# Up products of three feed-forwards by seven instead of eight block products, with the hidden values kept in DRAM until a separate down product

## Chip, cores and metric

The kernel runs on one core of a Trainium2 chip: TensorE (PE in the profile; PEld is its weight load) multiplies, VectorE (DVE), ScalarE (ACT) and GpSimd (POOL) do the elementwise work, SyncE (SP) issues most DMAs. Each engine takes its instructions in an order fixed when the program is built. The metric is the time of one execution on the device in microseconds (us), as the median of several runs.

## What is computed

Two transformer blocks in float32 on 1024 tokens of width 1024. Three feed-forwards of hidden width 2816 (22 tiles of 128) stand in it; the change touches these alone:

```
# block 1
h = rms_norm(x, g_pre_ffn[l]) * (1.0 + sc_f) + sh_f
up = dwconv3(h @ w_up[l], conv_w[l], conv_b[l])     # width 3 over the tokens
gate, val = jnp.split(up, 2, axis=-1)
y = (jax.nn.gelu(gate) * val) @ w_down[l]
x = x + gt_f * rms_norm(y, g_post_ffn[l])
# block 2, with ffn1 before its attention and ffn2 after it
def swiglu(x, w_gu, w_down):
    g, u = jnp.split(x @ w_gu, 2, axis=-1)
    return (jax.nn.silu(g) * u) @ w_down
h = h + 0.5 * rms_norm_2(f, ffn1_post_g[i])
```

Around them stand block 1's mixers (state space, Fourier, window attention), block 2's attention and its last gate (`ple`).

## The kernel before

Every float32 product is made of split pairs: a value is hi (rounded to the matmul's float32 format, `split`, by ACT) plus lo (the rest, by DVE), and `mm3` (L82) adds hi·hi, hi·lo and lo·hi in PSUM, so a product of 128x128 by 128x512 is three matmuls.

The activation h lies with its channels on the partitions, by token half: `hT` is two pairs of tiles [128, 8 k-tiles, 512 tokens]. `ffn` (L170) goes over the hidden width in groups of two tiles. A tile needs a gate and a value column block of 128 (`load_up`, one load of 512 KB, split on ACT and DVE), each for two token halves: four products of 8 k-tiles, 96 matmuls (`up`, `piece`). ACT applies silu (L241) or, in block 1, three taps and gelu (L184 to L205), DVE multiplies by the value and the result is split into `hidh`, `hidl` (L244, L206). The down product of the group before is put between the up products: `down` (L259) makes, for each of eight token tiles and two column halves, six matmuls in one PSUM bank, and DVE adds the bank to `yacc` in SBUF (L270). So hidden values never leave the core.

At its start the first two tiles' products are made by quarters of 256 tokens (`quarters`, L95), since h arrives token tile by token tile from the phase before, by transposes (L166) and splits (`hl<-tp` in the rows). At its end the down product of the last group completes the token tiles one by one; in between stand a few late up pieces. Each token tile then goes through `finish`: mean square on ACT (L126), multiplication by a row of gains on POOL (L132), a Newton iteration for the reciprocal root on DVE in 128x1 operations (L110 to L117), the residual (L1677), the next norm (L139) and its transposes.

The order in which the engines take the instructions is set by the program's scheduler from data dependences and from the rings of buffers: `wh`, `wl` a ring of four pairs for weights, `raw` a ring of three for loads, `mm` six PSUM banks.

## Time and profile before

| | |
|---|---|
| runs shown, us | 3457.92, 3458.81, 3458.82; median 3458.81 |
| span of the profiled execution, us | 3453.3; the runs' times hold some 5.5 us around it |
| PE busy | 3285.5 us, 95% of the span |
| DVE, ACT, POOL busy | 1849.3, 1060.3, 385.0 us |
| first feed-forward (block 1), about | 546 to 1255 us |
| second, third | 1309 to 2020, 2595 to 3300 us |

A row of the timeline gives the start of an instruction in us from the span's start, its length, engine, line, operation and tiles. A row of the windows gives for each engine the busy time and the number of instructions in a stretch, then the clock granted to TensorE as a share of full speed. A row of the groups gives the count, the busy time and the mean length of one in ns, then the engine's idle time before them and what ended it.

### The profile page before, as it was taken

Reading aid. Unit: us, or ns where it says so; the run is one execution under the profiler, and the core shown is the slowest. Engines: PE = TensorE matmul, PEld = TensorE weight load, DVE = VectorE, ACT = ScalarE, POOL = GpSimd, SP = SyncE. Lnnn points to the kernel's source line nnn. Section 1 sums busy time; section 2 is a strip of 40 time slices with the busy share of each in tenths; the row PEclk is TensorE's granted clock in tenths of the full one; section 3 lists DMA queues with packets and bytes.
Section 4 is the critical chain, followed back from the end, with each engine's and each line's share of the span. In section 5 each row is a group of like instructions: output and inputs, shape, how many; then the busy total and the mean of one; then the engine's idle time right before and its main releaser. Section 6 shows DMA issues by size and latency. Waiting matters only on the chain. (4 is left out here: it accounts for less than half of the span.)

```text
span 3453.3 us, 40957 instructions
## 1 busy us (share of the span) xinstructions
PE 3285.5 (95%) x16082; PEld 2648.9 (77%) x16082; DVE 1849.3 (54%) x3594; ACT 1060.3 (31%) x1717; POOL 385.0 (11%) x639
## 2 busy tenths in 40 slices
PE   5989888999999989999999989999999999999988
PEld 2766668888888878888888878777779888888866
DVE  7667497455554575233433387667673333333386
ACT  4335534322222223211111135446623111111142
POOL 3478331000000010000000020000020000000022
PEclk8999999999999999999999999999999999999999
DMA  7663543111111123111111132111632111111134
GB/s 204 178 216 116 171 162 119 43 49 49 48 38 55 49 92 98 46 47 49 43 49 49 49 116 85 43 47 66 227 110 74 49 49 49 49 46 47 43 134 146
DMA packets 263092, 293.67 MB, mean 85 GB/s; under 512 B 33448, under 2 KB 206760, under 8 KB 262899
## 3 DMA queue, kind: packets, MB, share of 16 engines
q1 hardware_dynamic: 254434, 276.52, 25.3%
q10 hardware_dynamic: 6576, 9.00, 0.8%
q0 software_dynamic: 1888, 5.53, 0.7%
q8 instruction: 127, 2.08, 0.3%
q14 instruction: 67, 0.54, 0.1%
HBM read 240.24 MB, written 57.06 MB: 86 GB/s over the span
## 5 line engine op out<-in xcount | busy, mean ns | idle before, releaser
L85 PE MATMUL mm<-hh,wh 128*128 128x512 f32 (+1 forms) x2800 | 1057.9, 378 | 15.7 <-ACT hh L47 15.7
L86 PE MATMUL mm<-hl,wh 128*128 128x512 f32 (+1 forms) x2800 | 1056.5, 377 | 3.5 <-DVE hl L48 3.5
L87 PE MATMUL mm<-hh,wl 128*128 128x512 f32 (+1 forms) x2800 | 1055.8, 377 | 0.8 <-DVE wl L48 0.8
L85 PEld LDWEIGHTS mm<-hh,wh 128*128 128x128 f32 x2800 | 529.6, 189 | 118.6 <-ACT hh L47 15.9
L86 PEld LDWEIGHTS mm<-hl,wh 128*128 128x128 f32 x2800 | 529.8, 189 | 105.5 <-DVE hl L48 3.9
L87 PEld LDWEIGHTS mm<-hh,wl 128*128 128x128 f32 x2800 | 529.7, 189 | 104.9 <-DVE wl L48 1.0
L270 DVE TENSOR_TENSOR y<-y,mm 128x512 f32<-128x512 f32 x480 | 324.0, 685 | 215.9 <-PE mm L87 215.5
L48 DVE TENSOR_TENSOR wl<-raw,wh 128x1024 fp32r<-128x1024 f32 x176 | 216.4, 1229 | 395.6 <-ACT wh L47 395.0
L85 PE MATMUL mm<-wdh,hidh 128*128 128x512 f32 x1056 | 414.6, 393 | 7.7 <-DVE tmp L190 5.8
L86 PE MATMUL mm<-wdl,hidh 128*128 128x512 f32 x1056 | 413.9, 392 | 0.0
L87 PE MATMUL mm<-wdh,hidl 128*128 128x512 f32 x1056 | 413.0, 392 | 0.0
L47 ACT ACTIVATE wh<-raw 128x1024 fp32r<-128x1024 f32 x178 | 188.1, 1058 | 604.8 <-PE mm L86 380.8
L243 DVE TENSOR_TENSOR tmp<-tmp,mm 128x512 f32<-128x512 f32 x88 | 60.4, 688 | 478.5 <-PE mm L87 477.4
L132 POOL TENSOR_TENSOR y<-y,row 128x1024 f32<-128x1024 f32 x24 | 59.3, 2475 | 2240.0 <-ACT junk L126 1516.8
L85 PEld LDWEIGHTS mm<-wdh,hidh 128*128 128x128 f32 x1056 | 199.0, 189 | 53.2 <-issue 6.6
L86 PEld LDWEIGHTS mm<-wdl,hidh 128*128 128x128 f32 x1056 | 199.3, 189 | 43.1 <-DVE wdl L48 0.2
L87 PEld LDWEIGHTS mm<-wdh,hidl 128*128 128x128 f32 x1056 | 198.7, 188 | 43.3
L47 ACT ACTIVATE wdh<-raw 128x1024 fp32r<-128x1024 f32 x66 | 66.8, 1054 | 419.8 <-issue 303.4
L47 ACT ACTIVATE hidh<-tmp 128x512 fp32r<-128x512 f32 (+2 forms) x111 | 78.8, 711 | 376.7 <-DVE tmp L243 230.0
L431 ACT ACTIVATE S<-S,m 128x257 f32<-128x257 f32 (+10 forms) x176 | 108.8, 620 | 93.6 <-DVE m L426 86.3
L132 POOL TENSOR_TENSOR tmp<-tmp,row 128x1024 f32<-128x1024 f32 x23 | 59.7, 2601 | 624.4 <-ACT junk L126 557.3
L116 DVE SCALAR_TENSOR_TENSOR rs_t<-rs_i,rs_a 128x1 f32<-128x1 f32 x288 | 124.7, 446 | 3.6
(332 smaller groups left out, 3915.6 us busy)
## 6 DMA issues: line engine op xcount, KB each, us to landing
raw<-in_ffn_w_gu SPq DMA_DIRECT2D x88, 512.0 KB, 3.9
raw<-in_w_ada SPq DMA_DIRECT2D x48, 512.0 KB, 3.8
raw<-in_w_up SPq DMA_DIRECT2D x44, 512.0 KB, 3.9
raw<-in_ffn_w_down SPq DMA_DIRECT2D x44, 512.0 KB, 3.8
x<-tmp SPq DMA_DIRECT2D x40, 512.0 KB, 2.6
tmp<-x SPq DMA_DIRECT2D x40, 512.0 KB, 5.1
raw<-in_w_in SPq DMA_DIRECT2D x28, 512.0 KB, 3.9
mix<-mix SPq DMA_DIRECT2D x44, 256.0 KB, 2.3
```

The source lines that it names most:

```text
L47: self.nc.scalar.activation(hi, src, AF.Copy)
L48: (eng or self.nc.vector).tensor_tensor(lo, src, f(hi), op=OP.subtract)
L85: mm(out, a[0], b[0], start=start, stop=False)
L86: mm(out, a[0], b[1], start=False, stop=False)
L87: mm(out, a[1], b[0], start=False, stop=stop)
L116: v.scalar_tensor_tensor(t, y, s, y, op0=OP.mult, op1=OP.mult)
L132: self.nc.gpsimd.tensor_tensor(y, y, row, op=OP.mult)
L243: v.tensor_tensor(s[:, c], s[:, c], p, op=OP.mult)
L270: v.tensor_tensor(yacc[i][:, c], yacc[i][:, c], po, op=OP.add)
L431: nc.scalar.activation(S[s][:, :ne], S[s][:, :ne], AF.Exp, scale=-1.0, bias=m[:, s:s + 1], accum_out=sm[:, s:s + 1])
```

## The change

`ffn` treats the first two hidden tiles as before, by quarters, but stores their hidden values in DRAM. Then it forms, once per call, sums of quarters of h. With the eight k-tiles in an upper and a lower half (A11, A12 for the first token half, A21, A22 for the second) these are S1 = A21 + A22, S2 = S1 - A11, S3 = A11 - A21 and S4 = A12 - S2, each split into hi and lo; POOL restores the quarters by adding hi and lo (L254), DVE makes the sums (L255 to L258), and S4 takes the place of A21. S1 to S3 lie in new tiles (`S`).

For each of the other 20 tiles the gate and the value block are loaded, POOL forms T1 to T4 from them (L268 to L277), and B11, B21, T1, T2, B22, T3 and T4 are split. Seven products of 4 k-tiles x 3 matmuls (`prod`, L287) go into three PSUM banks, A, B and C; bank A is copied out (ACT L319, L332) or read (DVE L338) between the products that it accumulates. T4's product of a tile is placed after B11's product of the next (`finish_tile`). The activation and the product of gate and value follow, and the hidden tile is stored in DRAM (L311).

When all are done, the down product runs as a phase of its own: pairs of hidden tiles and their weight rows are loaded and split (`load`), 96 matmuls per pair and a DVE add per bank (L368); the first pair is copied by ACT (L366). The last down takes four tiles at once, 24 matmuls per bank, and completes the token tiles one by one. Scratch tiles come from one ring of twelve (`b4`), rows and the sums `yacc` from the ring `S`; `ple` gets its weights' places from both.

```diff
-        return pool.tile([P, D], F32, name="tmp", tag="tmp", bufs=self.tmps)
+        return pool.tile([P, D], F32, name="tmp", tag=self.tmptag, bufs=self.tmps)
+    def places(self, pool, tag, n):
+        self.tmptag, self.tmps = tag, n
+    def count(self):
+        self.counted += 1
+        return self.counted
...
-def ffn(k, hT, w_gu, w_down, nff, prep, finish, G=2, taps=None, then=None):
...
+def ffn(k, hT, w_gu, w_down, nff, prep, finish, taps=None, then=None):
+    nc, v, pool = k.nc, k.nc.vector, k.nc.gpsimd
     with k.tc.tile_pool(name="ffn", bufs=1) as fp:
-        prep(fp)
-        yacc = [fp.tile([P, D], F32, name=f"y{i}") for i in range(NT)]
-        groups = [list(range(a, min(a + G, nff))) for a in range(0, nff, G)]
+        k.places(fp, "b4", 12)
+        hidden = k.dr.tile([nff, P, D], F32, name=f"hidden{k.count()}")
+        def b4(dt=F32):
+            return fp.tile([P, D], dt, name="b4", tag="b4", bufs=12)
+        def big(shape, dt):
+            return fp.tile([P] + shape, dt, name="S", tag="S", bufs=3)
+        state = {}
         def conv_half(U, p, m, h, edge):
...
+        def piece(j, part, h, p):
+            st = state.setdefault(j, {"left": 4})
...
+            c = slice(h * 512, h * 512 + 512)
...
+                if part not in st:
+                    st[part] = b4()
...
+                conv_half(st[part], p, j + part * nff, h, st[part, "e"])
+                if not st["left"]:
+                    s = st[0]
+                    nc.scalar.activation(s, s, AF.Gelu_apprx_tanh)
+                    v.tensor_tensor(s, s, st[1], op=OP.mult)
...
+                if "s" not in st:
+                    st["s"] = b4()
+                s = st["s"]
+                if part == 0:
+                    nc.scalar.activation(s[:, c], p, AF.Silu)
+                else:
+                    v.tensor_tensor(s[:, c], s[:, c], p, op=OP.mult)
+            if not st["left"]:
+                nc.sync.dma_start(hidden[j], s)
+        jobs = ((0, 0), (0, 1), (1, 0), (1, 1))
+        ws = [k.load_up(w_gu, (j + part * nff) * P) for j, part in jobs]
+        for h in range(2):
+            for x, ps in zip(jobs, k.quarters(ws, hT, h)):
+                piece(*x, h, ps)
+        (h0, l0), (h1, l1) = hT
+        sums = [big([2, 4, 512], F32R) for _ in range(3)]
+        up, dn = slice(0, 4), slice(4, 8)
+        A11, A12, A22, S4 = (h0[:, up], l0[:, up]), (h0[:, dn], l0[:, dn]), (h1[:, dn], l1[:, dn]), (h1[:, up], l1[:, up])
+        S1, S2, S3 = [(t[:, 0], t[:, 1]) for t in sums]
+        for a in range(0, 4, 2):
+            c = slice(a, a + 2)
+            x21, x22, x11, x12 = xs = [b4().rearrange("p (a b) -> p a b", a=2) for _ in range(4)]
+            for x, (hi, lo) in zip(xs, (S4, A22, A11, A12)):
+                pool.tensor_tensor(x, f(hi[:, c]), f(lo[:, c]), op=OP.add)
+            v.tensor_tensor(x22, x21, x22, op=OP.add)
+            v.tensor_tensor(x21, x11, x21, op=OP.subtract)
+            v.tensor_tensor(x11, x22, x11, op=OP.subtract)
+            v.tensor_tensor(x12, x12, x11, op=OP.subtract)
+            for x, (hi, lo) in ((x22, S1), (x11, S2), (x21, S3), (x12, S4)):
+                k.split(hi[:, c], lo[:, c], x)
+        def weights(j):
+            rg, rv = k.raw([P, 8, P]), k.raw([P, 8, P])
+            nc.sync.dma_start(rg, w_gu[:, j * P:j * P + P].rearrange("(k p) n -> p k n", p=P))
+            nc.sync.dma_start(rv, w_gu[:, (j + nff) * P:(j + nff) * P + P].rearrange("(k p) n -> p k n", p=P))
+            T = b4().rearrange("p (k n) -> p k n", k=8)
+            pool.tensor_tensor(T[:, up], rv[:, up], rg[:, up], op=OP.subtract)
+            W1 = [w.rearrange("p (k n) -> p k n", k=8) for w in k.wide()]
+            k.split(*W1, rg)
+            pool.tensor_tensor(T[:, dn], rv[:, dn], T[:, up], op=OP.subtract)
+            pool.tensor_tensor(rv[:, up], rv[:, dn], rv[:, up], op=OP.subtract)
+            W2 = [w.rearrange("p (k n) -> p k n", k=8) for w in k.wide()]
+            k.split(*W2, T)
+            W3 = [w.rearrange("p (k n) -> p k n", k=8) for w in k.wide()]
+            k.split(*W3, rv)
+            pool.tensor_tensor(T[:, up], rg[:, dn], T[:, dn], op=OP.subtract)
+            t4 = b4(F32R).rearrange("p (a k n) -> p a k n", a=2, k=4)
+            k.split(t4[:, 0], t4[:, 1], T[:, up])
+            both = lambda W, c: (W[0][:, c], W[1][:, c])
+            return dict(B11=both(W1, up), B21=both(W1, dn), T1=both(W2, up), T2=both(W2, dn), T3=both(W3, up),
+                        B22=both(W3, dn), T4=(t4[:, 0], t4[:, 1]))
+        def prod(ps, w, x, start):
+            for a in range(4):
+                for n, (y, z) in enumerate(((0, 0), (0, 1), (1, 0))):
+                    nc.tensor.matmul(ps, w[y][:, a], x[z][:, a], start=start and a == 0 and n == 0, stop=a == 3 and n == 2,
+                                     skip_group_check=True)
+        lo, hi = slice(0, 512), slice(512, 1024)
+        def finish_tile(j, A, w, s, V):
+            prod(A, w["T4"], A22, False)
+            if taps is None:
+                nc.scalar.activation(s[:, hi], A, AF.Silu)
+                v.tensor_tensor(s[:, hi], s[:, hi], V[:, hi], op=OP.mult)
+            else:
+                nc.scalar.activation(s[:, hi], A, AF.Copy)
+                us = []
+                for m, z in ((j, s), (j + nff, V)):
+                    u = b4()
+                    t = [taps[:, a, m:m + 1] for a in range(4)]
+                    nc.scalar.activation(u, z, AF.Identity, bias=t[3], scale=t[1])
+                    v.scalar_tensor_tensor(u[:, 1:], z[:, :D - 1], t[0], u[:, 1:], op0=OP.mult, op1=OP.add)
+                    v.scalar_tensor_tensor(u[:, :D - 1], z[:, 1:], t[2], u[:, :D - 1], op0=OP.mult, op1=OP.add)
+                    us.append(u)
+                s = us[0]
+                nc.scalar.activation(s, s, AF.Gelu_apprx_tanh)
+                v.tensor_tensor(s, s, us[1], op=OP.mult)
+            nc.sync.dma_start(hidden[j], s)
+        prev = None
+        for j in range(2, nff):
+            w = weights(j)
+            A, B, C = k.mm(), None, None
+            X = b4()
+            prod(A, w["B11"], A11, True)
+            nc.scalar.activation(X[:, lo], A, AF.Copy)
+            if prev is not None:
+                finish_tile(*prev)
+            s, V = b4(), b4()
+            B = k.mm()
+            prod(B, w["B21"], A12, True)
+            v.tensor_tensor(s[:, lo], B, X[:, lo], op=OP.add)
+            if taps is None:
+                nc.scalar.activation(s[:, lo], s[:, lo], AF.Silu)
+            C = k.mm()
+            prod(C, w["T1"], S1, True)
+            nc.scalar.activation(X[:, hi], C, AF.Copy)
+            prod(A, w["T2"], S2, False)
+            nc.scalar.activation(X[:, lo], A, AF.Copy)
+            prod(C, w["B22"], S4, False)
+            v.tensor_tensor(V[:, lo], C, X[:, lo], op=OP.add)
+            if taps is None:
+                v.tensor_tensor(s[:, lo], s[:, lo], V[:, lo], op=OP.mult)
+            prod(A, w["T3"], S3, False)
+            v.tensor_tensor(V[:, hi], A, X[:, hi], op=OP.add)
+            prev = (j, A, w, s, V)
+        finish_tile(*prev)
+        ys = [big([4, D], F32) for _ in range(2)]
+        yacc = [ys[i // 4][:, i % 4] for i in range(NT)]
+        def load(j):
+            r = k.raw([P, D])
+            nc.sync.dma_start(r, hidden[j])
+            h = b4(F32R), b4(F32R)
+            k.split(*h, r)
...
+            w = k.wide()
+            k.split(*w, r)
+            return h + w
+        def down(ready, first, last):
+            for i in range(NT):
...
                 for n in range(2):
...
+        n = nff - 4
+        for j in range(0, n, 2):
+            down([load(j), load(j + 1)], j == 0, False)
+        rows = big([4, D], F32)
+        k.rows = [rows[:, a] for a in range(3)]
+        k.junk = rows[:, 3]
+        prep(fp)
+        down([load(j) for j in range(n, nff)], False, True)
         k.close()
...
             then(fp)
+        k.rows = []
...
 def ple(k, pp, hT, e, w_gate, prep, finish):
...
-    places = [None] * 4 + [("y0", "y1", 1), ("y2", "y3", 1), ("hidh", "hidl", 3), ("y4", "y5", 1)]
-    for kt, tags in enumerate(places):
+    two = None
+    for kt in range(8):
...
+        if kt < 4:
             w = k.wide()
+        elif kt < 6:
+            if two is None:
+                two = pp.tile([P, 4, D], F32R, name="wg", tag="S", bufs=3)
+            w = two[:, 2 * kt - 8], two[:, 2 * kt - 7]
         else:
+            w = tuple(pp.tile([P, D], F32R, name=f"wg{kt}", tag="b4", bufs=12) for _ in range(2))
+    more = pp.tile([P, 4, D], F32, name="more", tag="S", bufs=3)
+    k.rows = [more[:, 0]]
+    k.junk = more[:, 1]
-        t = pp.tile([P, D], F32, name="e", tag="wdh", bufs=2)
+        t = pp.tile([P, D], F32, name="e", tag="b4", bufs=12)
-    k.junk = pp.tile([P, D], F32, name="junk", tag="y6", bufs=1)
```

How the order on the engines changes, at two places. On DVE at the start of the second feed-forward, from the last splits of h (`hl<-tp`), before:

```order
L48 TENSOR_TENSOR hl<-tp,hh 128x4x128 x2
L243 TENSOR_TENSOR tmp<-tmp,mm 128x512 x2
L71 TENSOR_SCALAR row<-row 128x1024
L48 TENSOR_TENSOR wdl<-raw,wdh 128x1024
L71 TENSOR_SCALAR row<-row 128x1024
L48 TENSOR_TENSOR hidl<-tmp,hidh 128x512 x2
L48 TENSOR_TENSOR wdl<-raw,wdh 128x1024
L48 TENSOR_TENSOR wl<-raw,wh 128x1024
```

and now the later part of what stands there (the numbered `b_` are scratch tiles of the ring; `S` the split sums):

```order
L257 TENSOR_TENSOR b_10850<-b_10849,b_10850 128x1024
L255 TENSOR_TENSOR b_10869<-b_10868,b_10869 128x1024
L258 TENSOR_TENSOR b_10851<-b_10851,b_10850 128x1024
L51 TENSOR_TENSOR S<-b_10850,S 128x1024
L51 TENSOR_TENSOR S<-b_10848,S 128x1024
L256 TENSOR_TENSOR b_10868<-b_10870,b_10868 128x1024
L51 TENSOR_TENSOR S<-b_10869,S 128x1024
L257 TENSOR_TENSOR b_10870<-b_10869,b_10870 128x1024
L51 TENSOR_TENSOR S<-b_10868,S 128x1024
L258 TENSOR_TENSOR b_10871<-b_10871,b_10870 128x1024
L51 TENSOR_TENSOR S<-b_10870,S 128x1024
L51 TENSOR_TENSOR wl<-raw,wh 128x1024
```

The first weight split of the next tile (`wl<-raw,wh`), which before came a few operations after the last split of h, now comes behind fourteen operations of the sums.

On DVE in the middle of the second feed-forward, before (a group's weights, activations and up splits; sixteen adds of L270 follow):

```order
L48 TENSOR_TENSOR wdl<-raw,wdh 128x1024 x2
L243 TENSOR_TENSOR tmp<-tmp,mm 128x512
L48 TENSOR_TENSOR hidl<-tmp,hidh 128x512
L48 TENSOR_TENSOR wl<-raw,wh 128x1024
L243 TENSOR_TENSOR tmp<-tmp,mm 128x512
```

and now, one tile (L338 is the read of bank A for the upper half of V):

```order
L325 TENSOR_TENSOR b_12052<-mm,b_12023 128x512
L334 TENSOR_TENSOR b_12053<-mm,b_12023 128x512
L336 TENSOR_TENSOR b_12052<-b_12052,b_12053 128x512
L51 TENSOR_TENSOR wl<-b_12127,wh 128x1024
L338 TENSOR_TENSOR b_12053<-mm,b_12023 128x512
L51 TENSOR_TENSOR wl<-raw,wh 128x1024
L51 TENSOR_TENSOR b_12144<-b_12127,b_12144 128x512
L51 TENSOR_TENSOR wl<-raw,wh 128x1024
L297 TENSOR_TENSOR b_12052<-b_12052,b_12053 128x512
```

The adds of the down product are gone from this place; the splits of the next tile's weight sums stand around the read of bank A.

## Rows read from the trace of the kernel before

**Rows 1.** The page: busy us, share of the span and instructions of each engine

```profile
span 3453.3 us, 40957 instructions
...
PE 3285.5 (95%) x16082; PEld 2648.9 (77%) x16082; DVE 1849.3 (54%) x3594; ACT 1060.3 (31%) x1717; POOL 385.0 (11%) x639
```

**Rows 2.** Windows inside the feed-forwards: PE, PEld, DVE, ACT, POOL, clock, DMA

```profile
700.00:750.00 50.00, 50.00 (x217) 40.54 (x216) 24.78 (x41) 13.82 (x16) 0.00 (x0) 1.00 0.21 63
1400.00:1450.00 50.00, 50.00 (x217) 40.45 (x216) 14.09 (x18) 8.74 (x12) 0.00 (x0) 1.00 0.18 56
2700.00:2750.00 50.00, 50.00 (x219) 40.72 (x218) 20.04 (x27) 8.08 (x11) 0.00 (x0) 1.00 0.14 43
```

**Rows 3.** Windows 1260-1324 (one, and the sum), 2020-2076 and 3300-3410 (sums)

```profile
1276.00:1280.00 4.00, 3.07 (x11) 2.56 (x11) 2.85 (x6) 0.56 (x2) 0.00 (x0) 0.50 0.93 284
...
sum 64.00, PE 50.91 PEld 44.76 DVE 61.17 ACT 28.63 POOL 14.80; mean PE 3.18 PEld 2.80 DVE 3.82 ACT 1.79 POOL 0.93
...
sum 56.00, PE 45.52 PEld 40.00 DVE 55.63 ACT 24.95 POOL 14.31; mean PE 6.50 PEld 5.71 DVE 7.95 ACT 3.56 POOL 2.04
...
sum 110.00, PE 93.28 PEld 73.51 DVE 99.37 ACT 43.00 POOL 28.42; mean PE 8.48 PEld 6.68 DVE 9.03 ACT 3.91 POOL 2.58
```

**Rows 4.** Groups by form, DVE and ACT: busy us, mean ns | idle before

```profile
L270 DVE TENSOR_TENSOR y<-y,mm 128x512 f32<-128x512 f32 x480 | 324.0, 685 | 215.9 <-PE mm L87 215.5
L48 DVE TENSOR_TENSOR wl<-raw,wh 128x1024 fp32r<-128x1024 f32 x176 | 216.4, 1229 | 395.6 <-ACT wh L47 395.0
...
L47 ACT ACTIVATE wh<-raw 128x1024 fp32r<-128x1024 f32 x178 | 188.1, 1058 | 604.8 <-PE mm L86 380.8 <-DMA raw<-in_ffn_w_gu 91.9 <-issue 73.0
...
L241 ACT ACTIVATE tmp<-mm 128x512 f32<-128x512 f32 x88 | 51.7, 589 | 166.7 <-PE mm L87 166.6
```

**Rows 5.** The same view, POOL's two-input instructions

```profile
L132 POOL TENSOR_TENSOR y<-y,row 128x1024 f32<-128x1024 f32 x24 | 59.3, 2475 | 2240.0 <-ACT junk L126 1516.8 <-DMA raw<-in_w_ple_gate 705.8 <-DVE rs_t L116 12.0
...
L1659 POOL TENSOR_TENSOR tmp<-tmp,row 128x512 f32<-128x512 f32 x1 | 1.3, 1292 | 3.2 <-DVE tmp L1622 3.2
```

**Rows 6.** The page's DMA issues (KB each, median us to landing)

```profile
raw<-in_ffn_w_gu SPq DMA_DIRECT2D x88, 512.0 KB, 3.9
...
x<-tmp SPq DMA_DIRECT2D x40, 512.0 KB, 2.6
```

**Rows 7.** Timeline in the first tail (start, length in us), DVE beside POOL

```profile
1252.74 4.79 POOL L132 TENSOR_TENSOR y<-y,row 128x1024 f32<-128x1024 f32 x2 [704.77 <-ACT junk L126]
1252.91 0.69 DVE L270 TENSOR_TENSOR y<-y,mm 128x512 f32<-128x512 f32 x1
...
1253.52 0.15 DVE L112 TENSOR_SCALAR rs_i<-rs_a 128x1 int32<-128x1 int32 x1
...
1253.70 1.47 DVE L116 SCALAR_TENSOR_TENSOR rs_t<-rs_i,rs_a 128x1 f32<-128x1 f32 x1
...
1255.20 2.33 DVE L117 SCALAR_TENSOR_TENSOR rs_i<-rs_t,rs_i 128x1 f32<-128x1 f32 x1
```

**Rows 8.** Timeline, the last split of h before each feed-forward

```profile
554.85 1.29 DVE L48 TENSOR_TENSOR hl<-tp,hh 128x512 fp32r<-128x512 f32 x2 [0.84 <-ACT hh L47]
...
1327.34 1.29 DVE L48 TENSOR_TENSOR hl<-tp,hh 128x512 fp32r<-128x512 f32 x2 [1.44 <-ACT hh L47]
...
2603.74 1.29 DVE L48 TENSOR_TENSOR hl<-tp,hh 128x512 fp32r<-128x512 f32 x2 [1.44 <-ACT hh L47]
```

**Rows 9.** Timeline, the first full-width up product after the quarters of each feed-forward

```profile
587.68 0.39 PE L85 MATMUL mm<-hh,wh 128*128 128x512 f32 x1
...
1351.39 0.39 PE L85 MATMUL mm<-hh,wh 128*128 128x512 f32 x1
...
2637.64 0.39 PE L85 MATMUL mm<-hh,wh 128*128 128x512 f32 x1
```

**Rows 10.** Timeline, the residual of token tiles 3 and 7 in the first tail

```profile
1291.45 1.28 DVE L1677 SCALAR_TENSOR_TENSOR tmp<-y,rs_i,tmp 128x1024 f32<-128x1024 f32 x1
...
1317.38 1.28 DVE L1677 SCALAR_TENSOR_TENSOR tmp<-y,rs_i,tmp 128x1024 f32<-128x1024 f32 x1
```

More of the change, by code (lines that the diff above doesn't have):

```diff
@@ L36, in __init__ @@
         self.tail = None
+        self.rows = []
+        self.tmptag = "tmp"
+        self.counted = 0
     def raw(self, shape):
@@ L236, in piece @@
-            c = slice(h * 512, h * 512 + 512)
-            if "s" not in st:
-                st["s"] = k.tmp(fp)
-            s = st["s"]
-            if part == 0:
-                nc.scalar.activation(s[:, c], p, AF.Silu)
-            else:
-                v.tensor_tensor(s[:, c], s[:, c], p, op=OP.mult)
-                k.split(hh[:, c], hl[:, c], s[:, c])
-        def up(j):
-            order = ((0, 0), (0, 1), (1, 0), (1, 1)) if taps is not None else ((0, 0), (1, 0), (0, 1), (1, 1))
-            for part, h in order:
-                piece(j, part, h)
@@ L256, in down_w @@
-            k.split(wh, wl, r)
-            return state[j]["hid"] + (wh, wl)
-        def down(ready, tiles, first, last):
-            for i in tiles:
+            w = k.wide()
[3 more added lines that the diff above has]
+            for i in range(NT):
                 t = slice(i * P, i * P + P)
@@ L274, in down @@
                         k.flush(2, 1)
-        a, b = groups[0]
-        jobs = ((a, 0), (a, 1), (b, 0), (b, 1))
-        for h in range(2):
-            for x, ps in zip(jobs, k.quarters([weight(*x) for x in jobs], hT, h)):
-                piece(*x, h, ps)
-        every = range(NT)
-        n = len(groups)
-        for gi in range(n - 2):
-            ready = [down_w(j) for j in groups[gi]]
-            up(groups[gi + 1][0])
-            down(ready, every, gi == 0, False)
-            for j in groups[gi + 1][1:]:
-                up(j)
-        a, b = groups[-1]
-        ready = [down_w(j) for j in groups[-2]]
-        if taps is None:
-            early, late, n = ((a, 0, 0), (a, 1, 0), (b, 0, 0), (b, 1, 0)), ((b, 0, 1), (b, 1, 1)), 4
-        else:
-            early, late, n = ((a, 0, 0), (a, 0, 1), (a, 1, 0), (a, 1, 1), (b, 0, 0), (b, 1, 0)), ((b, 0, 1), (b, 1, 1)), 3
-        for x in early:
-            piece(*x)
-        down(ready, every, False, False)
-        ready = [down_w(j) for j in groups[-1]]
-        k.junk = fp.tile([P, D], F32, name="junk", tag="hidh", bufs=G + 1)
-        if taps is None:
-            piece(a, 0, 1)
-            piece(a, 1, 1)
-        down(ready, every[:n], False, True)
-        for x in late:
-            piece(*x)
-            k.flush(2, 1)
-        down(ready, every[n:], False, True)
+        n = nff - 4
[6 more added lines that the diff above has]
+        down([load(j) for j in range(n, nff)], False, True)
         k.close()
@@ L685, in project @@
     nc = k.nc
-    k.tmps, k.nrows = 4, nrows
+    k.places(None, "tmp", 4)
+    k.nrows = nrows
     with k.tc.tile_pool(name="proj", bufs=1) as pp:
```

44 lines of the change are left out of this document (1 added, 43 removed).

## Prediction

> **What bounds the kernel now.** I read the page's engine line first: TensorE (PE) is busy 3285.5 of 3453.3 us, VectorE (DVE) 1849.3, ScalarE (ACT) 1060.3, GpSimd (POOL) 385.0 [rows 1]. Then windows inside each feed-forward: PE is busy for the whole 50 us at granted clock 1.00, with 217 to 219 matmuls of 128x512 in each, so one takes 50/217 = 0.230 us [rows 2]; DVE and ACT fill half or less. So in the feed-forwards the time is the number of matmuls, and a matmul that goes is 0.23 us off the end. Last, windows over the ends of the three feed-forwards. There PE is busy 50.91 of 64, 45.52 of 56 and 93.28 of 110 us, so it idles 13.1, 10.5 and 16.7 us while DVE is busy nearly throughout, and after an idle stretch the granted clock stands at 0.50 (the lower level, 1.2 GHz): 11 matmuls in 4 us [rows 3]. I put 3 us on each such recovery. These ends are the second resource: here DVE and POOL set the time.
>
> **What it removes.** A tile of the hidden width took 2 parts x 2 token halves x 8 k-tiles x 3 = 96 matmuls; by seven products it takes 7 x 4 x 3 = 84. 20 of 22 tiles change, in three calls: 12 x 20 x 3 = 720 matmuls, and 720 x 0.230 = **-166 us**. The down product keeps its count.
>
> **The steady tile.** 84 x 0.230 = 19.3 us of PE. Beside it DVE gets, in the silu calls, 3.5 low-part splits of a 128x1024 weight at 1.23 us and five half-tile operations at 0.69 = 7.7 us; in the convolution call 3.5 splits, five two-input passes of the whole width (four taps, one product) at 1.23 and three half-tile adds = 12.5 us. ACT gets 3.5 high parts at 1.06, four or five copies or activations of a half at 0.59 and in the convolution three passes of 1.06: below 10 us [rows 4]. POOL gets four 128x512 operations at 1.29 = 5.2 us [rows 5]. Even if POOL and DVE took strict turns, 12.5 + 5.2 = 17.7 < 19.3. The one short dependence is on PSUM bank A: T4 of a tile must wait until DVE has read A for V's upper half, and only B11 of the next tile, 12 x 0.230 = 2.8 us, stands between; the read costs 0.69 and nothing later than it is queued ahead of it on DVE (the W2 split ahead belongs to work done half a tile before). SyncE (SP) now has a store of the hidden tile between a tile's two weight loads, so the second load waits for the activation's end; it still lands, at 3.9 us [rows 6], some 15 us before its first product. So I cost the steady tile at nothing beyond its matmuls; without that cover the price is in the third rival.
>
> **The down phase.** Nine pairs of 96 matmuls, 22.1 us each, against DVE's 16 adds at 0.685 and 4 splits at 1.23 = 15.9 us [rows 4]. The next pair's loads and splits are placed between the adds of this one. Nothing added. At the change of phase, the last tile has no next tile to cover it. In the convolution its chain is T4, copy, taps, gelu, and the next instructions on DVE, the first pair's splits, queue behind: about 4 x 1.23 + 2 x 1.06 + 0.69 = 7.7, say +8. In the silu calls other down products stand in between: +2 each. The last down product holds four pairs of weights, all four places of the ring; two of them come free only when the pair before ends: one load's split, 1.5 us, per call, +4.5. Sum **+16**, bounds 0 (all hidden) and 30 (3.9 us of load and 2.3 of split in sight at each of four places, and a clock recovery).
>
> **The transform of h.** It needs all of h, so it starts at the last split, 556.1, 1328.6 and 2605.0 us [rows 8], and PE has only the rest of the quarters to do: the first product after them stood at 587.7, 1351.4 and 2637.6 [rows 9]. Cover: 31.6, 22.8 and 32.6 us. The work: POOL adds hi and lo eight times at 2.475 = 19.8 us [rows 5]; DVE has eight two-input operations, six low-part splits and then the split of the first weight, which stands behind them in its order: 15 x 1.23 = 18.5 us [rows 4]. Whether these run side by side decides. In the first tail POOL's two multiplications run from 1252.74 to 1257.53; a DVE add with one operand in PSUM (0.69) and a one-input operation (0.15) run beside them at their own length, but a 128x1 operation with two SBUF operands takes 1.47 us and ends with POOL's first, and the next takes 2.33 and ends with POOL's second [rows 7]. So they take turns, and 19.8 + 18.5 = 38.3 us is the length of the chain.
>
> The Trainium skill, page "SBUF — State Buffer", section "Who interferes with whom", states the same rule as an exclusive lock: a DVE instruction with two SBUF inputs and a GpSimd instruction that reads SBUF block each other for the whole instruction. It speaks against splitting the transform over these two engines, and by it the chain is the sum; without it, it would be the longer of the two, as in the first rival. The rows above agree with it, at 1.47 and 2.33 us.
>
> Place by place. First call: DVE also has the eight convolution passes of the first half-tiles ahead of the transform and those of the second half in it, so W1's low part is ready about 44 us after 556.1 and W2's, behind four more splits, at 55 to 58; PE has 5.5 us of B11 and B21 in between: stall 18 to 22, take 20. Second: 38.3 + 1.4 for two value pieces (0.69 each) in between - 22.8 = 17. Third: the quarters of the second half, 192 matmuls of half the width, 22.1 us, begin 10.5 us after 2605.0, so a value piece of the first half holds DVE until some 11 us in, while POOL gets on alone with about half its adds; 11 + 14 x 1.23 + 4 x 2.475 = 38.1, less 32.6: 6. Each is idle long enough to drop the clock, +3. **+52**; bounds 11 (side by side: 8 + 3 + 0) and 90 (each 40 us chain starts 4 us late behind the stores of x and pays ACT's hand-over in each of six splits).
>
> **The ends.** Before, the PE work from the first finished token tile is about 30 us (late up pieces and the down of the rest); now the last down gives 192 x 0.230 = 44.2 us with the first token tile after 5.5, so 38.7. The finish goes on at its pace of (1317.38 - 1291.45)/4 = 6.5 us per token tile [rows 10], slower than 5.5, so it still ends last, but 8 us more of it are covered: 3 x -8 = **-24**; bounds 0 (the next phase's weights can't be split before the ring's places are free, at the end of the last down) and -33.
>
> **Sum.** -166 + 16 + 52 - 24 = -122 us. From the profiled span, 3453.3 - 122 = 3331; the median of the runs shown, 3458.8, is 5.5 above that span, so **3337 us**.
>
> **Rivals.** (1) *The transform is hidden*: the two engines overlap after all, or the order gives PE other work. For it: the adds could run while DVE waits for PSUM. Against: rows 7. Starts 11 instead of 52: 3296. (2) *The starts cost their upper bound*, and the down phase too: +38 and +14: 3389. For it: the chain crosses three engines eight times. (3) *Slower than before*: the weight sums on POOL come late in every tile. If the second weight load, behind the hidden store on SP, lands less than a tile ahead, POOL's four sums, ACT's high part and DVE's low part (5.2 + 1.06 + 1.23 = 7.5 us) stand ahead of the read of bank A, and past the cover of 2.8 each tile loses 4.7 us: 60 x 4.7 = 282, 3619 us. It decides from 122/60 = 2.0 us per tile on. Against: the 15 us of slack and 17.7 < 19.3. (4) *The saving is not there*: the seven products, with a new stationary tile per matmul and three banks in turn, run no faster per tile than 96; only starts and ends move, +44: 3503. Against: before too changes the stationary tile each matmul, at 0.230 us.
>
> **How the numbers follow.** Forecast 0.58, rival 1 0.18, rival 2 0.15, rival 3 0.05, rival 4 0.02, and 0.02 for a stall that just eats the gain. Range: from a little below rival 1 to rival 2, **3285 to 3395**; it leaves out 3 and 4 and the tails. A measurement tells 0.2%, 7 us, from no change: faster 0.91, same 0.02, slower 0.07.
>
> **What would show it.** Windows in the changed up phase: PE busy throughout, 84 matmuls per 19.3 us; a stall ahead of the first product of bank A of each tile would be rival 3. After the quarters: a hole in PE of 20, 17 and 6 us, ended by DVE's W1 or W2 split, with POOL and DVE busy in turns; no hole is rival 1. The down phase: 22.1 us per pair. The ends: 8 us less idle in each. Wrong above all if the three holes together are far from 43 us, or if matmuls come at another rate than 0.230.

## The result and the profile after

The changed kernel takes 3306.1 us (median of four runs, 3302.0 to 3310.4) against 3458.8: a ratio of 0.9557, 95% interval 0.9544 to 0.9571. The forecast was 3337 with a range of 3285 to 3395: the sign and the main term held, the gain is 153 us in place of 122. By the number alone the first rival, 3296, is nearer than the forecast; what speaks against it is its mechanism (e1). The changed kernel's runs spread over 8 us, those of before over about 1, so below some 4 us one profile of it tells nothing. The profiled execution spans 3304.9 us, 148.4 less than before; its own time is 2.0 above its span, where 5.5 had been assumed. (The later runs of the kernel before, whose times and spans are both on record, are 1.8 to 2.4 apart. So the 5.5 compared a median with the span of another execution, and the profile of before is of one some 3.5 us faster than its median: 148 by spans and 153 by times are the same gain.) All sums below are of spans.

Busy time by engine, as in [rows 1]:

```profile
span 3304.9 us, 40845 instructions
...
PE 3122.3 (94%) x15362; PEld 2525.5 (76%) x15362; DVE 2131.3 (64%) x3648; ACT 1274.2 (39%) x1975; POOL 791.7 (24%) x903
```

PE has 15362 matmuls, 720 fewer, and is 163.2 us less busy; DVE has 282 us more to do, POOL 407 (waiting inside an instruction counts as busy). PE still fills 94% of the span: the new elementwise work lies beside it almost everywhere.

Windows of the changed kernel, columns as in [rows 2]: up products of the first (convolution) and the second (silu) call, then a stretch of the second call's down phase.

```profile
700.00:1000.00 300.00, 298.82 (x1285) 241.62 (x1283) 194.37 (x183) 139.36 (x165) 75.27 (x57) 1.00 0.26 83
1350.00:1650.00 300.00, 300.00 (x1303) 244.15 (x1302) 129.22 (x140) 103.43 (x140) 83.28 (x61) 1.00 0.25 79
1725.00:1865.00 140.00, 140.00 (x619) 115.95 (x618) 94.04 (x125) 29.84 (x32) 0.00 (x0) 1.00 0.31 99
```

PE has no idle slice in a silu call's steady part. The products of a tile start every 19.37 us in both silu calls and every 19.52 us in the convolution, 18 tiles in a row without a deviation of 0.01; a pair of the down phase takes 21.76. DVE is busy 0.65 of the time in the convolution call and 0.43 in the silu call, and PE sets the pace in both. (The first window's missing 1.2 us are matmul records that the trace lacks: its tiles follow each other at 19.52 us like the others.)

Where PE does wait is after the quarters. Timeline rows of PE, with the idle time before an instruction and what ended it in brackets, call by call:

```profile
594.19 0.50 PE L287 MATMUL mm<-hh,wh 128*128 128x512 f32 x1 [1.86 <-ACT wh L50]
...
602.12 0.80 PE L287 MATMUL mm<-hh,wl 128*128 128x512 f32 x1 [7.19 <-DVE wl L51]
...
615.62 1.20 PE L287 MATMUL mm<-S,wh 128*128 128x512 f32 x2 [1.96 <-ACT b L319]
...
1315.37 0.79 PE L287 MATMUL mm<-hh,wh 128*128 128x512 f32 x1 [5.70 <-ACT wh L50]
...
1317.87 0.79 PE L287 MATMUL mm<-hh,wl 128*128 128x512 f32 x1 [1.29 <-DVE wl L51]
...
1332.27 0.50 PE L287 MATMUL mm<-hh,wh 128*128 128x512 f32 x1 [1.55 <-ACT b L330]
...
2547.53 0.73 PE L287 MATMUL mm<-hh,wh 128*128 128x512 f32 x1 [2.90 <-ACT wh L50]
...
2550.04 0.80 PE L287 MATMUL mm<-hh,wl 128*128 128x512 f32 x1 [1.34 <-DVE wl L51]
```

Most of the idle time is ended by W1, the split of the tile's first weight block (ACT its high part, DVE its low part). But some 1.5 to 2 us in each call are a wait of another kind, for ACT's copy of a PSUM bank (L319, L330; in the third call 1.53 us at 2564.43). The same stretches as windows; the clock column is below 1.00 because each hole is followed by a time at the lower level:

```profile
592.00:616.00 24.00, 12.34 (x44) 8.94 (x44) 22.13 (x32) 15.19 (x18) 3.25 (x1) 0.78 0.12 46
1308.00:1334.00 26.00, 17.46 (x71) 13.42 (x70) 20.26 (x17) 12.78 (x17) 9.86 (x5) 0.80 0.24 81
2543.00:2569.00 26.00, 20.23 (x82) 15.68 (x82) 18.82 (x19) 13.38 (x17) 7.89 (x4) 0.87 0.24 81
```

### The profile page after: what moved, and what is told of

Same layout as the page of the kernel before. It is cut to its first block, busy times and chain, and to the rows that moved or that the text cites. A ratio compares the mean times of both kernels' runs of the same rounds, so it can differ in the third digit from the quotient of the medians.

```text
span 3304.9 us, 40845 instructions
## 1 busy us (share of the span) xinstructions
PE 3122.3 (94%) x15362; PEld 2525.5 (76%) x15362; DVE 2131.3 (64%) x3648; ACT 1274.2 (39%) x1975; POOL 791.7 (24%) x903
## 5 line engine op out<-in xcount | busy, mean ns | idle before, releaser
L287 PE MATMUL mm<-S,wh 128*128 128x512 f32 x1440 | 448.3, 392 | 2.0 <-ACT b L319 2.0
L88 PE MATMUL mm<-wh,b 128*128 128x512 f32 x1056 | 414.2, 393 | 4.0 <-ACT b L50 4.0
L89 PE MATMUL mm<-wl,b 128*128 128x512 f32 x1056 | 413.3, 392 | 0.0
L90 PE MATMUL mm<-wh,b 128*128 128x512 f32 x1056 | 412.6, 391 | 0.3 <-DVE b L51 0.3
L368 DVE TENSOR_TENSOR S<-S,mm 128x512 f32<-128x512 f32 x432 | 289.0, 684 | 127.6 <-PE mm L90 127.1
L287 PEld LDWEIGHTS mm<-S,wh 128*128 128x128 f32 x1440 | 271.5, 189 | 62.9 <-ACT b L319 2.4
L88 PE MATMUL mm<-hh,wh 128*128 128x256 f32 (+1 forms) x880 | 300.7, 342 | 16.5 <-ACT hh L50 16.5
L90 PE MATMUL mm<-hh,wl 128*128 128x256 f32 (+1 forms) x880 | 298.0, 340 | 4.8 <-DVE wl L51 4.8
L89 PE MATMUL mm<-hl,wh 128*128 128x256 f32 (+1 forms) x880 | 299.0, 340 | 3.5 <-DVE hl L51 3.5
L287 PE MATMUL mm<-hh,wh 128*128 128x512 f32 x720 | 286.8, 398 | 13.5 <-ACT wh L50 10.5
L287 PE MATMUL mm<-hh,wl 128*128 128x512 f32 x720 | 287.4, 399 | 9.8 <-DVE wl L51 9.8
L287 PE MATMUL mm<-hl,wh 128*128 128x512 f32 x720 | 286.3, 398 | 0.0
L287 PE MATMUL mm<-S,wl 128*128 128x512 f32 x720 | 282.2, 392 | 0.7 <-DVE wl L51 0.7
L334 DVE TENSOR_TENSOR b<-mm,b 128x512 f32<-128x512 f32 x60 | 41.5, 692 | 330.5 <-PE mm L287 329.3
L88 PEld LDWEIGHTS mm<-wh,b 128*128 128x128 f32 x1056 | 200.1, 190 | 45.8 <-ACT b L50 4.5
L90 PEld LDWEIGHTS mm<-wh,b 128*128 128x128 f32 x1056 | 199.3, 189 | 43.3 <-DVE b L51 1.8
L277 POOL TENSOR_TENSOR b<-raw,b 128x512 f32<-128x512 f32 x60 | 79.7, 1329 | 582.5 <-DVE wl L51 582.5
```

Source lines behind the costliest of these rows:

```text
L88: mm(out, a[0], b[0], start=start, stop=False)
L89: mm(out, a[0], b[1], start=False, stop=False)
L90: mm(out, a[1], b[0], start=False, stop=stop)
L277: pool.tensor_tensor(T[:, up], rg[:, dn], T[:, dn], op=OP.subtract)
L287: nc.tensor.matmul(ps, w[y][:, a], x[z][:, a], start=start and a == 0 and n == 0, stop=a == 3 and n == 2, skip_group_check=True)
L334: v.tensor_tensor(V[:, lo], C, X[:, lo], op=OP.add)
```

## Experiments

All are edits of the changed kernel. Times are medians of four or five runs, beside 3306.1 of the changed kernel; e7 is one run.

### e1: the adds of the transform on DVE

```diff
-                pool.tensor_tensor(x, f(hi[:, c]), f(lo[:, c]), op=OP.add)
+                v.tensor_tensor(x, f(hi[:, c]), f(lo[:, c]), op=OP.add)
```

> The changed kernel with one edit: the eight adds of hi and lo at the start of each feed-forward run on DVE instead of POOL; the rest is as it was. Theory (DVE and POOL take turns on two-input operations, so the transform is a sum): the chain loses 8 x 2.475 us of POOL and gains 8 x 1.21 on DVE, W1's low part is ready some 30 us after the last split of h instead of 38, and the holes in PE after the quarters (15.7, 11.7 and 8.9 us with the clock recovery, 36 together) shrink to about 10 together: some 3280 us against 3306. Rival (the two engines run side by side and DVE's own list is the chain): eight more operations on DVE lengthen it by 9.7 us in each call, the holes grow to 65: some 3335.

Measured: 3288.5 us (3286.4 to 3291.5), ratio to the kernel before 0.9505 (0.9489 to 0.9521). More work on the busier engine made the kernel 18 us faster, so the rival falls for the kernel as a whole. First the changed kernel, POOL and DVE at the start of its second call (the last split of h ends at 1279.87):

```profile
1279.49 23.75 POOL L254 TENSOR_TENSOR b<-hh,hl 128x1024 f32<-128x1024 f32 x8 [17.71 <-DVE hl L51]
```

```profile
L254 POOL TENSOR_TENSOR b<-hh,hl x8: 2395/3368/3409, 1279.5 to 1299.9; 128x1024 f32<-128x1024 f32 x8
```

```profile
1278.58 1.29 DVE L51 TENSOR_TENSOR hl<-tp,hh 128x512 fp32r<-128x512 f32 x2 [0.84 <-ACT hh L50]
...
1284.27 3.39 DVE L255 TENSOR_TENSOR b<-b,b 128x1024 f32<-128x1024 f32 x1 [2.30 <-POOL b L254]
1287.59 0.68 DVE L234 TENSOR_TENSOR b<-b,mm 128x512 f32<-128x512 f32 x1
...
1290.92 3.40 DVE L51 TENSOR_TENSOR S<-b,S 128x1024 fp32r<-128x1024 f32 x1
...
1316.61 1.21 DVE L51 TENSOR_TENSOR wl<-raw,wh 128x1024 fp32r<-128x1024 f32 x1
```

POOL's eight adds follow each other at 2.97 us on the mean, not 2.475: the last row gives the shortest, the median and the longest in ns, 2.4 us for the three that no two-input operation of DVE stands beside, 3.4 for the other five. DVE's two-input operations beside them take 3.4 in place of 1.2, about one POOL add and itself; the one with an operand in PSUM (L234) keeps its 0.68. Then e1's DVE at the same place:

```profile
1277.40 1.29 DVE L51 TENSOR_TENSOR hl<-tp,hh 128x512 fp32r<-128x512 f32 x2 [0.84 <-ACT hh L50]
...
1286.53 1.22 DVE L254 TENSOR_TENSOR b<-hh,hl 128x1024 f32<-128x1024 f32 x1
...
1301.29 1.22 DVE L51 TENSOR_TENSOR wl<-raw,wh 128x1024 fp32r<-128x1024 f32 x1
```

Each takes 1.22, and W1's split starts 22.6 us after h is complete (1301.29 - 1278.69) instead of 36.7. The windows of e1 at the three starts:

```profile
592.00:616.00 24.00, 12.75 (x39) 9.04 (x38) 20.65 (x25) 9.60 (x11) 3.27 (x1) 0.64 0.20 72
1308.00:1334.00 26.00, 25.50 (x115) 20.52 (x114) 18.52 (x18) 11.13 (x15) 9.43 (x7) 1.00 0.34 101
2533.00:2559.00 26.00, 25.49 (x114) 20.58 (x114) 18.98 (x18) 11.25 (x15) 8.78 (x7) 1.00 0.35 101
```

In the silu calls the holes of 9 to 12 us, clock included, are gone: the first tile's six products take 17.4 us where 16.6 are the matmuls. In the convolution call nothing was won (719.1 us from its h to the next call's, against 719.2), which the expectation had not seen. There the rival holds in part: W1's low part is ready 47.1 us after h in place of 41.4, since DVE's own list is the chain: rows of e1's DVE, which hardly pauses from 568 to 611 us (taps of the classic tiles in between), and the PE row that waits for it:

```profile
568.04 1.22 DVE L254 TENSOR_TENSOR b<-hh,hl 128x1024 f32<-128x1024 f32 x1
...
605.50 1.22 DVE L51 TENSOR_TENSOR wl<-raw,wh 128x1024 fp32r<-128x1024 f32 x1
```

```profile
606.78 0.80 PE L287 MATMUL mm<-hh,wl 128*128 128x512 f32 x1 [8.30 <-DVE wl L51]
```

### e2 and e5: a third classic tile as cover

e2 makes a third tile by the four classic products ahead of the transform, in all calls. e5 does so in the convolution call alone, and has e1's edit as well.

```diff
+        w3 = [k.load_up(w_gu, (2 + part * nff) * P) for part in range(2)]
+        for part, h in (((0, 0), (0, 1), (1, 0), (1, 1)) if taps is not None else ((0, 0), (1, 0), (0, 1), (1, 1))):
+            p = k.mm()
+            k.up(p, w3[part], hT[h])
+            piece(2, part, h, p)
...
-        for j in range(2, nff):
+        for j in range(3, nff):
```

> The changed kernel with a third hidden tile of each feed-forward by the classic four products at full width, placed ahead of the transform of h, and 19 tiles by seven products. Theory (the holes are a cover that is too short): each call pays 22.4 - 19.4 = 3.0 us more matmuls and gets 22 us more cover; the holes go from 36 to some 5 together: 3306 + 9 - 31 = 3284. Rival (the holes come from the order of instructions on DVE, which the extra tile's pieces push back as well): holes stay, 3306 + 9 = 3315.

Measured: 3295.8 us (3294.5 to 3299.8). In the silu calls no hole is left (the first tile's products take 16.6 us, the bare matmuls), at 3.0 us a call for the extra matmuls; in the convolution the first tile still takes 30.9 us against 30.5, and only the 1.9 us of waiting ahead of it are gone. So the theory holds where PE's cover is what is short, and the rival holds in the convolution call. By the traces: -21 + 9 = -12, near the 10 measured.

> The adds of hi and lo on DVE in all three calls (as in e1_adds_dve), and a third classic tile in the convolution call alone, where that run left a hole of 12.2 us and 17 us at the lower clock. Theory (cover and a shorter chain add up): the convolution call pays 2.8 us of matmuls and gets 22 us of cover, its hole and the lower clock, 12.2 + 8.5, go: 3288.5 + 2.8 - 20.7 = 3271. Rival (in the convolution DVE is held by the taps of the classic tiles, which the third tile adds to): the hole stays, 3291.

Measured: 3300.3 us (3298.4 to 3303.5), 12 slower than e1 and 9 above the rival's 3291. So the rival has the direction, and falls short: the hole did not stay, it grew. The convolution call takes 727.5 us from h to h in place of e1's 719.1; 2.8 of it are the tile's matmuls, and PE stands idle for 15.2 us behind the third tile, where e1 has 11.2. The tile's taps and splits stand on DVE's list ahead of the transform, and PE waits for it later. (The 20.7 us that the theory hoped for counted idle time twice: of e1's 11.2 idle us 9.0 lie inside the 17 us at the lower clock, so its hole cost some 15.) The two longest waits of PE in e5 after the third tile:

```profile
622.12 1.22 PE L295 MATMUL mm<-S,wh 128*128 128x512 f32 x2 [3.91 <-ACT wh L50]
631.44 0.79 PE L295 MATMUL mm<-S,wl 128*128 128x512 f32 x1 [8.10 <-DVE wl L51]
```

### e10 and e11: two mixtures for the convolution call

Both keep e1's edit in the silu calls. In the convolution call e10 puts the first four adds on POOL and the last four on DVE; e11 puts all on POOL and adds the third classic tile there.

```diff
# e10
-                pool.tensor_tensor(x, f(hi[:, c]), f(lo[:, c]), op=OP.add)
+                (pool if taps is not None and a == 0 else v).tensor_tensor(x, f(hi[:, c]), f(lo[:, c]), op=OP.add)
# e11
+                (v if taps is None else pool).tensor_tensor(x, f(hi[:, c]), f(lo[:, c]), op=OP.add)
```

> Adds of hi and lo on DVE in the two silu calls; in the convolution call the first four on POOL, the last four on DVE; no third classic tile. Theory (DVE's own list is the chain in the convolution call, and POOL's adds are free only while DVE works on operands in PSUM, as it does on the taps there): four operations of 1.21 us leave DVE's list, the hole shortens by some 5 us: 3283 against 3288.5. Rival (POOL's 2.475 us each hold DVE up for longer than they spare it): 3288 to 3294.

> Adds on DVE in the two silu calls; in the convolution call all eight on POOL and a third classic tile. Theory (the hole of the convolution call is as in e2_third_tile, 7.6 us and 10 us at the lower clock, against 12.2 and 17 in e1_adds_dve): 3288.5 + 2.8 - 8 = 3283. Rival (the third tile costs by more than its matmuls, as in e5_dve_third_conv): 3290 to 3300.

Measured: e10 3284.9 us (3283.7 to 3292.7, ratio 0.9502, 0.9486 to 0.9517), e11 3291.6 (3288.2 to 3293.4). In e10 PE is idle for 11.2 us after the first call's quarters, as in e1, and from the first call's h to the second's it takes 718.6 us in place of 719.1: the splitting did next to nothing, and most of the difference lies before the first call, 2.9 us in the two profiles. So e10's median is near its theory's 3283 without its mechanism, which is luck. POOL's four adds did run alone there, at 2.40 us each. But DVE began its part 11.3 us after h, where e1's begins at 8.4, and W1's low part was ready only 0.8 us sooner, 46.3 after h against 47.1. e1 and e10 can't be told apart; they beat the changed kernel by 18 and 21 us. e11's median lies in its rival's range, and the trace bears the rival out: PE's idle time falls from 11.2 to 9.3 us, but with the third tile's matmuls the call takes 721.5 us, 2.4 more than e1's.

### e4: the separate down phase alone

All 22 tiles by the classic products, hidden values through DRAM, down product as a phase. The transform, the weight sums and the seven products are left out (their removed lines are not shown).

```diff
+        order = ((0, 0), (0, 1), (1, 0), (1, 1)) if taps is not None else ((0, 0), (1, 0), (0, 1), (1, 1))
         for j in range(2, nff):
...
+            w = [k.load_up(w_gu, (j + part * nff) * P) for part in range(2)]
+            for part, h in order:
+                p = k.mm()
+                k.up(p, w[part], hT[h])
+                piece(j, part, h, p)
```

> One part of the change alone: hidden values through DRAM and the down product as a phase of its own, but all 22 tiles by the classic four products (96 matmuls, no transform of h, no sums of weights). Theory (the gain is the matmuls, at the spacing that the traces show for them: 22.4 us a classic tile in silu, 22.3 in the convolution, against 19.37 and 19.52): 20 x (3.0 + 3.0 + 2.8) = +177 us, and the holes after the quarters go, -36: 3447 us, so 12 below the kernel before. By the step of the prediction, 12 x 0.230 per tile: +166 - 36, 3436. Rival (the separate down phase is itself worth much of the gain): below 3420.

Measured: 3439.2 us (3437.3 to 3443.3), ratio 0.9941 (0.9926 to 0.9956): this half of the change is worth 20 us of the 153, and the products the other 133. There is no hole after the quarters. Windows of its second call, up and down:

```profile
1400.00:1700.00 300.00, 300.00 (x1288) 241.30 (x1287) 51.70 (x54) 44.19 (x55) 0.00 (x0) 1.00 0.23 71
1830.00:1970.00 140.00, 140.00 (x620) 115.91 (x619) 97.85 (x131) 27.07 (x27) 0.00 (x0) 1.00 0.33 98
```

The up phase gives 1288 matmuls in 300 us, 0.233 each, where the changed kernel has 1303. The median lies between the two expectations, 3447 and 3436, and alone decides nothing; the calls do. From h to h the silu calls take 49.5 and 50.4 us more than the changed kernel's. With 3.03 us a tile and the holes gone that is 60.6 - 11.6 = 49.0 and 60.6 - 8.9 = 51.7; with 12 x 0.230 it would be 43.6 and 46.3. The convolution call takes 33.3 more, against 56.0 for its tiles less 15.7 for the hole and some 7 for the change of phase, where PE has no idle time in e4.

### e7: twice the work on POOL

```diff
             pool.tensor_tensor(T[:, up], rg[:, dn], T[:, dn], op=OP.subtract)
+            for _ in range(4):
+                pool.tensor_tensor(T[:, up], rg[:, dn], T[:, dn], op=OP.subtract)
```

> The changed kernel with POOL's last weight sum of each tile issued four times more, so POOL has eight 128x512 operations per tile in place of four. Theory (turns in the steady tile too): DVE 12.5 + POOL 10.3 = 22.9 us exceed the 19.5 us of PE in the convolution call, +3.4 us a tile there, +65 in all; in the silu calls 7.7 + 10.3 = 18.0 stay below 19.4, nothing: some 3370 us. Rival (no turns, POOL alone far from full): no change in any call, 3306 to 3312.

Measured: 3359.4 us (one run). A convolution tile takes 20.97 us, +1.45, and a silu tile 19.62, +0.25. So the rival falls. The size, +3.4 and 0, was wrong, and so is the reasoning behind it: DVE is not full (222.71 of 300 us in the first window, the waits inside its instructions included), so what costs time is no sum of both engines' work but a chain through them. Windows of e7; then rows of one convolution tile; then the summary of ACT's copy L334 (L332 of the changed kernel), with its waits and who waited for it, in us and times:

```profile
700.00:1000.00 300.00, 283.76 (x1205) 225.18 (x1204) 222.71 (x170) 131.68 (x160) 179.19 (x116) 1.00 0.24 76
1400.00:1700.00 300.00, 299.97 (x1287) 240.13 (x1286) 160.22 (x138) 95.77 (x138) 197.35 (x125) 1.00 0.25 81
```

```profile
757.14 7.15 POOL L279 TENSOR_TENSOR b<-raw,b 128x512 f32<-128x512 f32 x4
...
764.32 0.63 ACT L50 ACTIVATE b<-b 128x512 fp32r<-128x512 f32 x1 [6.87 <-POOL b L279]
...
767.24 3.54 DVE L307 SCALAR_TENSOR_TENSOR b<-b,taps,b 128x1023 f32<-128x1023 f32 x2 [1.15 <-ACT b L306]
```

```profile
L334 ACT ACTIVATE b<-mm x14: 597/597/598, 710.9 to 983.6; 128x512 f32<-128x512 f32 x14
...
  DVE b L327: 10.3, 14
...
  PE mm L289: 16.2, 14
```

This is the mechanism of the third rival in small. The repeated sums take POOL 7.15 us: two of the four take 2.16 in place of 1.30, beside DVE's splits, so turns are taken in the steady tile too. ACT waits for the last of them with the split of T4 (6.87 us here), and behind that split in its order stands the copy that the taps need (L301). So DVE's taps come late, and with them the add L327, which reads what the copy L334 will overwrite. L334 waits for that add, and PE waits for L334, 16.2 us in 14 tiles. How much of the 1.45 us a tile is due to the turns and how much to the longer work alone is open. 7.15 us more of POOL cost 1.45, so in the convolution call the change stands at most some three such operations from this edge (an estimate from this one run).

### e8: a shorter last down product

```diff
-        n = nff - 4
+        n = nff - 2
```

> The changed kernel, but the last down product takes two tiles instead of four, so 96 matmuls lie under the finish of the token tiles in place of 192. Theory (the finish, at 6.5 us per token tile, needs cover): PE work behind the first finished token tile falls from 38.7 to 19 us in each of three calls, +20 each: 3306 + 59 = 3365. Rival (the ends wait for the next phase's weights, whose places in the ring the last down holds; two places are now free early): no change or a few us less, 3295 to 3306.

Measured: 3343.8 us (3338.6 to 3346.8), +38. From h complete to the next h complete the calls take 17.6, 16.5 and 21.5 us more, close to the 20 expected; but the last phase, from its h to the end of the kernel, takes 56.3 us in place of 72.6, and gives 16.3 back. So the theory has the calls, and neither expectation has the whole. DVE's rows for h complete in the second call and in the last phase, and PE's first product after the second call's quarters:

```profile
1297.22 1.37 DVE L51 TENSOR_TENSOR hl<-tp,hh 128x512 fp32r<-128x512 f32 x2 [0.78 <-ACT hh L50]
...
3284.79 1.28 DVE L51 TENSOR_TENSOR hl<-tp,hh 128x512 fp32r<-128x512 f32 x2
```

```profile
1333.94 0.80 PE L287 MATMUL mm<-hh,wh 128*128 128x512 f32 x1 [10.25 <-ACT wh L50]
```

### e9: no transform

S1, S2, S3 and S4 are taken to be A11, A12, A22 and A21; the sums of h are left out.

```diff
-        sums = [big([2, 4, 512], F32R) for _ in range(3)]
...
-        S1, S2, S3 = [(t[:, 0], t[:, 1]) for t in sums]
+        S1, S2, S3 = A11, A12, A22
...
-        for a in range(0, 4, 2):
...
```

> The changed kernel without the transform of h: no sums, S1 to S3 are the quarters A11, A12, A22 and S4 is A21, all matmuls stay; the output is another. Theory (the transform costs its holes and little else): the holes of 15.7, 11.7 and 8.9 us go, 3306 - 36 = 3270. Beside it a question that no theory of mine settles: matmuls that read h took 0.2333 us in the silu calls, those that read S 0.2275. If that goes with the tile, a silu tile now takes 84 x 0.2333 = 19.6 us, +0.2 a tile and +9 in all (3279); if it goes with the values or the product, 19.4.

Measured: 3282.9 us (3280.7 to 3286.3). All holes are gone, and a silu tile takes 19.60 us = 84 x 0.2333, so in the silu calls the spacing goes with the tile that is read. Window of its second call:

```profile
1350.00:1650.00 300.00, 300.00 (x1287) 241.37 (x1286) 126.68 (x140) 101.95 (x139) 83.33 (x61) 1.00 0.25 79
```

1287 matmuls in place of 1303. By the profiles the three calls take 15.0, 4.8 and 3.9 us less, 23.7 together, where the holes and the spacing (-36 and +9) give 27. This profile has 3.7 us more before the first call, and is 20.4 us shorter in all; the medians differ by 23.2.

## Why the prediction was right, step by step

| term | forecast, us | measured, us |
|---|---|---|
| matmuls | -166 | -182 |
| change of phase, last down's weights | +16 | +8 |
| holes after the quarters | +52 | +36 |
| ends of the calls | -24 | -34, and +20 given back in the phases behind |
| before the first call | 0 | +4 |
| sum of spans | -122 | -148 |

The forecast was right in its mechanisms, and its sum is in part luck. The first four terms each came out lower than forecast, by 50 us together; 24 us that no term had were lost again, so the sum misses by 26. The -34 is no measurement of its own: it is what the other terms leave (below), and holds their errors.

**Matmuls: right mechanism, the price of one mis-sized.** 0.230 us was a mean over two kinds. In the trace of before the down product of a pair begins at the first row, the next two tiles' up products at the second, the next down at the third:

```profile
1440.29 0.39 PE L85 MATMUL mm<-wdh,hidh 128*128 128x512 f32 x1
...
1462.07 0.40 PE L85 MATMUL mm<-hh,wh 128*128 128x512 f32 x1
...
1506.86 0.39 PE L85 MATMUL mm<-wdh,hidh 128*128 128x512 f32 x1
```

96 down matmuls in 21.78 us are 0.2269 each, 192 up matmuls in 44.79 are 0.2333. The changed silu tile has 48 at about 0.233, which read h, and 36 at 0.2275, which read S, so it saves 3.03 us and not 2.76: 2 x 20 x 3.03 = 121. In the convolution call two tiles with their down took 66.9 us and now take 2 x 19.52 + 21.76 = 60.8: 10 x 6.1 = 61. Only the row of one phase would have shown this, not the 50 us window of the mixture. The rates and call times of e4 and the rates of e9 agree.

**The steady tile at nothing: right.** 19.37 and 19.52 us without a hole; the elementwise work fitted under PE. The bound of 17.7 us, DVE and POOL in turns, is not what would have broken first: in e7 it was a chain through POOL, ACT and DVE.

**Change of phase: +16 was too much.** In the convolution call PE waits three times, for the read of bank A and for the first pair's high and low parts:

```profile
996.56 0.50 PE L287 MATMUL mm<-hh,b 128*128 128x512 f32 x1 [0.78 <-DVE b L338]
...
1003.64 0.50 PE L88 MATMUL mm<-wh,b 128*128 128x512 f32 x1 [4.04 <-ACT b L50]
...
1007.60 0.77 PE L90 MATMUL mm<-wh,b 128*128 128x512 f32 x1 [0.28 <-DVE b L51]
```

That is 5.1 us, and with 3.4 us at the lower clock behind it some 7 of the 8 put on it. In the silu calls it is 0.3, and the last down's weights cost nothing that a row shows.

**The transform: right in mechanism, and almost in length.** W1's low part was ready 37.95 us after h in the second call (1316.61 + 1.21 - 1279.87) and 38.1 in the third, against 38.3 + 1.4 and 38.1 (the third's sum has 14 operations of DVE where the second's has 15); 41.4 in the first against 44. e1 and e9 show the cause and the cost. What was too large is the holes, 15.7, 11.6 and 8.9 with the clock's share, against 23, 20 and 9: the second call's quarters ended 29.6 us after h, not 22.8 (below), and W2 followed W1 closer than I had counted. ACT's copies of banks, 1.5 to 2 us a call, were not in the forecast's holes.

**The ends: more than forecast, and then less.** These rows and [rows 8] give h complete, after: 560.6, 1279.9, 1983.2 (attention), 2511.9 and 3232.3 us (the last phase):

```profile
559.34 1.29 DVE L51 TENSOR_TENSOR hl<-tp,hh 128x512 fp32r<-128x512 f32 x2 [2.10 <-ACT hh L50]
...
1981.91 1.29 DVE L51 TENSOR_TENSOR hl<-tp,hh 128x512 fp32r<-128x512 f32 x2 [1.44 <-ACT hh L50]
...
2510.57 1.29 DVE L51 TENSOR_TENSOR hl<-tp,hh 128x512 fp32r<-128x512 f32 x2 [1.44 <-ACT hh L50]
...
3230.97 1.29 DVE L51 TENSOR_TENSOR hl<-tp,hh 128x512 fp32r<-128x512 f32 x2 [0.24 <-ACT hh L50]
```

and before, for the attention and the last phase, 2080.6 and 3389.3:

```profile
2079.22 1.37 DVE L48 TENSOR_TENSOR hl<-tp,hh 128x512 fp32r<-128x512 f32 x2 [0.84 <-ACT hh L47]
...
3388.59 0.69 DVE L48 TENSOR_TENSOR hl<-tp,hh 128x512 fp32r<-128x512 f32 x1 [0.16 <-ACT hh L47]
```

Taking the matmuls, the holes and the change of phase out of the intervals from the end of the quarters to the next h, 14.9, 6.9 and 12.5 us were won, 34 together. But the next phase did not start on it: the second call's quarters end 6.8 us later after h than before, the attention up to the third call's h takes 528.7 us against 524.4, and the last phase 72.6 against 64.0. So 20 us went back to what waits behind the end, and the ends net 14 of the 24 forecast. e8 shows the same from the other side: with two places of the weights' ring free, the quarters of its second call end 24.9 us after h, attention takes 525.7, the last phase 56.3. In the second call, though, an early end of the quarters is worth little: e8's first product behind them starts 35.4 us after h (1333.94 - 1298.59), the changed kernel's 35.5, since both wait for W1; what the quarters lose there the hole gains. So most of the 6.8 us would have been hole. That the places are what the next phase waits for is only argued; no run changed them alone. A later h also leaves the last phase less to do after it.

**Rivals.** The first (side by side) fell with e1, though its 3296 is nearer to the result than the forecast: the price of the holes was real, only the second call's cover longer. The second falls with holes of 36 us in place of 90. The third has its mechanism, in e7, and was at most some three POOL operations per tile away. The fourth is excluded by 84 matmuls in 19.37 us. The 4 us before the first call were not tried. The experiments' profiles have 0.5 to 8.2 there, and none of their edits stands in that stretch, so it is likely the spread between executions.

## What to carry to other kernels

Price a removed instruction by the phase that it leaves, not by a window that mixes phases: here 0.2333 against 0.2269 us made a tenth of the gain. Before elementwise work is shared between DVE and POOL, look for an instruction of one that ends with one of the other; where they take turns, the slower engine's share is better done by the faster (e1: 18 us for one word), unless the faster engine is itself the chain. What is won at the end of a phase counts only if the next phase can start on it; that its first weights wait for buffers which the ending phase still holds is the place to look first, and here it is argued, not shown.
